# Roots and reciprocals of the heads' norms as columns of 128 tokens x 4, laid out and spread by small DMAs on ScalarE's queue

## The chip, the cores and the metric

The kernel runs on one core of a Trainium2 chip. A core has engines that run side by side, each with its own in-order queue: TensorE (PE; its weight loads are shown as PEld), VectorE (DVE), ScalarE (ACT), GpSimd (POOL) and SyncE (SP, here only for issuing DMAs). Sixteen DMA engines move data between the chip's memory and the core's. The metric is the device time in microseconds of one execution; the profile is of one execution.

## The reference

One sequence of 512 tokens of width 1024 in float32 passes two layers. Each layer is a token mixer and a convolutional FFN, both behind an RMS norm with a shift, a scale and a gate that come from a conditioning vector. Layer 0 mixes by retention, layer 1 by mLSTM, each with 4 heads of width 512. Both end with a norm over each head's 512 values of a token, and here lies the change:

```python
def head_groupnorm(y, g):
    mu = jnp.mean(yf, axis=-1, keepdims=True)
    var = jnp.mean((yf - mu) ** 2, axis=-1, keepdims=True)
    yn = (yf - mu) * lax.rsqrt(var + EPS)
    return yn.reshape(Bt, S, -1) * g
```

In the mLSTM, what is normed is `num / max(|den|, exp(-m_row))` times a sigmoid. A factor per token cancels in the norm except beside EPS, so the kernel norms the numerators alone and adds EPS times the square of the denominator to the variance. Per head and token there is one root and one reciprocal: 512 numbers per head, 8 heads.

## The kernel before

Activations lie transposed, features on the 128 partitions and the 512 tokens along the row. A sum over features is then a matmul with a matrix of ones, and its result comes out repeated on all 128 partitions, as a tile of 128x512. Weights and activations are split in a high and a low part, and each product is three matmuls; the low parts are made by VectorE, or by ScalarE and an accumulating DMA that GpSimd issues (`low_part_added`, L484). Many projections use a seven-product scheme (`seven`, L799), in which each step's result goes through a ScalarE copy into `fs` and a VectorE addition into `p`.

All instructions are first recorded as `Call` objects, then put in order by a planner (`Plan`, L144) and issued, so that nearly every instruction carries the line of `Plan.issue` (L377). The planner simulates the engines with a cost for each instruction (`occ`, the time on its engine; `dma`, the time of a transfer), gives each call a due time worked back from the TensorE instruction that needs it, and for each engine takes the most urgent call that its simulation finds ready. The resulting order of each engine is fixed. Conditioning columns (`side_work`, L457) are loaded into `ada` by SyncE and reduced by VectorE in between.

`heads` (L1296) writes down the order of TensorE's work in a layer's heads, with `q`, `v` and `g` for projections, `s` for the scores, `a` for the attention, `o` for the output projection (four pieces a head, each 24 full matmuls), and `end` for the head's norm. `between` functions put a call after the j-th step of a projection. In `q` and `g` a head has 14 steps of 12 matmuls, in `v` 7 steps of 24. `boundary` (L1046) runs the last pieces in two halves of 256 tokens, so that the next norm can begin. `RET_LAST` and `ML_LAST` (L43) set where the last head's steps stand among the pieces.

`gn_root` (L1285) sums the squares by two matmuls with ones into the bank `pvar`, takes the root (ScalarE) and the reciprocal (VectorE) of the whole 128x512 tile `grs`, and `ret_end` and `ml_end` multiply the head's four tiles `z` by it and split them into `y` (`yh`, `yl`). In an mLSTM head `ml_attend` (L1806) sums the scores into the bank `pden`, and makes from it the tile `den`: absolute value (ScalarE), maximum with `db` (VectorE), square (ScalarE). `db` is one row of `scratch`, a buffer in the chip's memory, spread to 128 partitions by a DMA of SyncE. `bcols` holds another quantity of the gates as columns: 128 tokens on the partitions, 4 columns per head.

Of the kernel before, what the change touches and what calls it, by code (L numbers as in the profile page):

```python
# [16 lines left out]
P = 128  # L17
# [120 lines left out]

class Call:
    __slots__ = ("eng", "name", "obj", "a", "k", "bufs", "preds", "succs", "occ", "lat", "dma", "due", "left", "ready",  # L140
                 "new", "fn", "pin", "after", "end", "shared")


class Plan:  # L144
# [14 lines left out]
    def add(self, eng, obj, name, a, k):  # L159
        c = Call()  # L160
        c.eng, c.obj, c.name, c.a, c.k = eng, obj, name, a, k
        c.preds, c.succs, c.fn, c.pin, c.after = set(), [], None, self.pin, None
        n = len(self.calls)
        views = [(v, m == 0) for m, v in enumerate(a) if isinstance(v, View)]
        views += [(v, key == "accum_out") for key, v in k.items() if isinstance(v, View)]
        c.bufs = list({id(v.buf): v.buf for v, _ in views}.values())
        for v, w in views:
            self.note(n, c, v, w)
        c.dma = 0.0
# [84 lines left out]
        return self.run()  # L254

    def tail(self, c):
        return c.lat if not c.dma else c.dma + (4.5 if "accum_op" in c.k else 3.0)

    def run(self):
        calls = self.calls  # L260
# [58 lines left out]
        while len(out) < len(calls):  # L319
# [61 lines left out]
def trunk(ctx: ExitStack, tc: tile.TileContext, xT, cb, pos, vec, ident, decay, zmask, ada, w_s0, w_in0, w_v0,  # L381
# [811 lines left out]
    class End(Norm):  # L1193
# [24 lines left out]
        def rest(self):  # L1218
# [3 lines left out]
            for k in range(0, KT, 2):  # L1222
                item([], lambda w, k=k: self.use(1, k, k + 2))

    def scores(q, k, hd, weigh, total=None):

        out_s = []
# [54 lines left out]
            V.tensor_tensor(z[:], z[:], ps[:], op=ALU.subtract)  # L1282
        gn_squares(st)

    def gn_root(st, extra=None):  # L1285
        ps = bank("pvar")
        mm2(ps[:], ones["v"][:], st["sum"])
        rs = slot("grs")
        if extra is None:
            reciprocal_root(rs, ps[:], slice(None), eps_t[:])  # L1290
        else:
            V.tensor_tensor(rs[:], ps[:], extra[:], op=ALU.add)
            reciprocal_root(rs, rs[:], slice(None), 0.0)
        st["rs"] = rs

    def heads(st, q, v, s, g, a, mid, end, o, norm, at_last):  # L1296

        def on(fn, i):
            return lambda: item([], lambda w: fn(i))
        S, A_, mid_, end_ = (lambda i, f=f: on(f, i)() for f in (s, a, mid, end))  # L1300
        def at(where, fn, i):
            return lambda j: fn(i) if j == where else None

        q(0)
        q(1, at(6, S, 0))
# [24 lines left out]
    def gate_col(layer, which):  # L1330
        base = (16, 40)[which]
# [193 lines left out]

    def ret_end(i):
        st = R[i]
        gn_root(st)
        st["y"] = []
        for vt in range(4):  # L1530
            z = st["z"][vt]
# [169 lines left out]
                proj_item(w_in0[i * 8 + 2 * n + j], h0, then)  # L1701
        item([], lambda w: sums_early())

    def ret_g(i):
        fold_pairs(pair_srcs(w_in0, i * 8 + 4), sums0.terms, [ret_gate(i)] * 2)

    def ret_v(i, between=nothing):
        fold_values(w_v0[i - 1], sums0.terms, R[i]["v"], center_split, between)
# [6 lines left out]
    def ret_o(i):  # L1715
        if not i:
# [4 lines left out]
    heads(R, ret_q, ret_v, ret_scores, ret_g, ret_attend, lambda i: None, ret_end, ret_o,  # L1721
          ffn0.start, RET_LAST)
# [5 lines left out]
    bcols = fixed(const, [P, 4, H], F32, "bcols")  # L1728
    zm = fixed(const, [P, P], F32, "zm")

    def gates(ps):
# [45 lines left out]

    def ml_scores(i):
        st = M[i]
        mb, db = slot("mb"), slot("db")  # L1780
        S.dma_start(mb[:], scratch[i : i + 1].broadcast_to([P, T]))
        S.dma_start(db[:], scratch[4 + i : 5 + i].broadcast_to([P, T]))

        def weigh(p, ps, J, lo, n):
            w = slot("w")
# [11 lines left out]
        st["db"] = db  # L1797

    def ml_gate(i):
        def then(ps):  # L1800
# [5 lines left out]
    def ml_attend(i):  # L1806
# [6 lines left out]
        gn_sum(st)  # L1813
        ps = bank("pden")
        mm2(ps[:], ones["1"][:], st["sums"])
        d = slot("den")
        A.activation(d[:], ps[:], AF.Abs)
        V.tensor_tensor(d[:], d[:], st["db"][:], op=ALU.max)
        A.activation(d[:], d[:], AF.Square, scale=float(np.sqrt(EPS)))
        st["e2"] = d  # L1820

    def ml_end(i):
        st = M[i]
        gn_root(st, st["e2"])
        st["y"] = []
        for vt in range(4):
            z = st["z"][vt]
# [12 lines left out]
    def ml_g(i):  # L1840
        fold_pairs(pair_srcs(w_in1, 5 + i * 8), start1.sums.terms, [ml_gate(i)] * 2)

    def ml_o(i):
        return pieces(lambda j: w_o1[i, j], 4, gate_col(1, 0), lambda k: M[i]["y"][k], i in O_ADDED)
# [1 line left out]
    def ml_v(i, between=nothing):  # L1846
# [5 lines left out]
    v_items(w_v1, 0, h1, M[0]["v"], plain_split)  # L1852
    item([], lambda w: start1.sums.turn())
    ffn1 = Ffn(1)
    heads(M, ml_q, ml_v, ml_scores, ml_g, ml_attend, lambda i: gn_center(M[i]), ml_end, ml_o,
          ffn1.start, ML_LAST)
    ffn1.items(End())


# [143 lines left out]
```

## Time and profile before

| | |
|---|---|
| median of 3 executions | 1513.67 us |
| lowest, highest | 1513.44, 1513.98 us |
| the profiled execution | 1513.25 us |
| its span, first to last instruction | 1511.3 us |
| granted TensorE clock, mean | 0.994 |

In the profile `DVE RECIPROCAL grs<-grs` names engine, operation, and the tile written and the tiles read; x8 is a count. A row of a busy-time table gives a stretch of time, its length, the busy time and count of instructions of PE, PEld, DVE, ACT and POOL, then the granted TensorE clock (1.00 is full), the busy share of the DMA engines and GB/s. A row of waits reads: who waited, for whom, total us, times, longest. A row of the timeline reads: start, duration, engine, operation, tiles, count, and in brackets the idle time of the engine before it and who ended it. A row of one tile's instructions gives the shortest, median and longest duration in ns and the first and last start. SPq is SyncE issuing DMAs. Matmul rows overlap, since matmuls are pipelined.

### The profile page before, as it was taken

How to read it: one execution, taken by the hardware profiler on the slowest of the kernel's cores; microseconds unless marked ns; L12 is line 12 of the kernel's file. 1: busy time of each engine (PE TensorE's matmuls, PEld its weight loads, DVE VectorE, ACT ScalarE, POOL GpSimd, SP SyncE). 2: the span in 40 equal slices, each digit the busy share in tenths (PEclk: the TensorE clock that was granted, in tenths of full speed). 3: DMA queues.
4: the chain of work that ended last, by engine and by line, in shares of the span. 5: the costliest groups of instructions: out<-in, count | busy, mean ns of one | idle time of the engine just before them, and what ended most of it. 6: DMA issues, size and time to landing. Idle time of an engine off the chain costs nothing.

```text
span 1511.3 us, 27097 instructions
## 1 busy us (share of the span) xinstructions
PE 1477.9 (98%) x10405; PEld 1375.5 (91%) x10405; DVE 1262.9 (84%) x2123; ACT 1069.0 (71%) x1593; POOL 281.6 (19%) x311
## 2 busy tenths in 40 slices
PE   9999999899999999999999999999999999999997
PEld 6889999798998989899998988999989899999997
DVE  6998989676887888888798999999877877877786
ACT  4558858777577666666578986899976867677662
POOL 0234222232111111111001222223131111111100
PEclk9999999999999999999999999999999999999999
DMA  9467999896487999999368887989875868787841
GB/s 375 158 161 204 282 272 275 207 236 148 103 224 202 244 265 255 271 260 253 115 168 223 206 234 202 262 216 248 223 179 136 213 171 196 173 207 182 204 127 56
DMA packets 92979, 314.98 MB, mean 208 GB/s; under 512 B 12193, under 2 KB 14625, under 8 KB 92850
## 3 DMA queue, kind: packets, MB, share of 16 engines
q0 software_dynamic: 31824, 115.88, 41.4%
q1 hardware_dynamic: 61026, 197.38, 36.7%
q8 instruction: 81, 1.33, 0.3%
q14 instruction: 48, 0.39, 0.1%
HBM read 195.23 MB, written 2.12 MB: 131 GB/s over the span
## 4 chain that ended last, share of the span: by engine, by line
PE 85%; DVE 6%; DMA 6%; ACT 2%; issue 1%; POOL 0%; SPq 0%; DVEq 0%; ACTq 0%; POOLq 0%
PE p L377 31%; PE po L377 25%; PE pv L377 9%; PE pp L377 6%; PE pf L377 4%; PE pav L377 4%; PE pst L377 3%; PE psc L377 2%; DMA wb<-w_up 1%; DMA ada<-ada 1%; PE pc L377 1%; ACT whi L377 1%; DVE ws L377 1%; DVE wlo L377 1%; DVE ada L377 1%
## 5 line engine op out<-in xcount | busy, mean ns | idle before, releaser
L377 PE MATMUL p<-hh,whi 128*128 128x256 f32 (+1 forms) x962 | 267.8, 279 | 5.8 <-DVE p L377 5.5
L377 PE MATMUL p<-hl,whi 128*128 128x256 f32 x960 | 266.8, 278 | 0.7 <-DVE hl L377 0.5
L377 PE MATMUL p<-hh,wlo 128*128 128x256 f32 x960 | 265.3, 278 | 1.5 <-DMA wlo<-wa 1.5
L377 ACT ACTIVATE wlo<-whi 128x1024 fp32r<-128x1024 f32 x221 | 233.2, 1059 | 45.5 <-PE po L377 22.0
L377 PEld LDWEIGHTS p<-hh,whi 128*128 128x128 f32 x962 | 181.5, 189 | 7.7 <-DVE p L377 6.0
L377 PEld LDWEIGHTS p<-hl,whi 128*128 128x128 f32 x960 | 181.3, 189 | 1.5 <-DVE hl L377 1.1
L377 PEld LDWEIGHTS p<-hh,wlo 128*128 128x128 f32 x960 | 180.3, 189 | 2.0 <-DMA wlo<-wa 1.9
L377 PE MATMUL p<-t24h,whi 128*128 128x256 f32 x720 | 161.3, 281 | 6.9 <-DVE p L377 4.2
L377 DVE SCALAR_TENSOR_TENSOR x<-po,mod,x 128x512 f32<-128x512 f32 (+1 forms) x184 | 113.6, 629 | 52.5 <-PE po L377 51.7
L377 PE MATMUL po<-ggh,wlo 128*128 128x512 f32 (+1 forms) x448 | 152.6, 343 | 0.8 <-DVE wlo L377 0.8
L377 PE MATMUL po<-ggl,whi 128*128 128x512 f32 (+1 forms) x448 | 153.1, 343 | 0.0
L377 PE MATMUL po<-ggh,whi 128*128 128x512 f32 (+1 forms) x448 | 152.6, 343 | 0.0
L377 ACT CAST whi<-raw 128x1024 fp32r<-128x1024 f32 (+1 forms) x121 | 121.8, 1019 | 26.0 <-PE po L377 7.8
L377 PE MATMUL p<-t24l,whi 128*128 128x256 f32 x480 | 133.6, 278 | 0.0
L377 PEld LDWEIGHTS p<-t24h,whi 128*128 128x128 f32 x720 | 123.0, 189 | 10.8 <-DVE p L377 5.9
L377 DVE SCALAR_TENSOR_TENSOR ada<-ada,c_ext 128x1025 f32<-128x1025 f32 x96 | 122.0, 1275 | 10.4 <-DMA ada<-ada 10.4
L377 POOL DMA_DIRECT2D wlo<-wa x60 | 53.0, 883 | 414.7 <-ACT wlo L377 320.1
L377 PE MATMUL po<-yh,whi 128*128 128x256 f32 (+1 forms) x354 | 116.0, 329 | 0.0
L377 PE MATMUL po<-yl,whi 128*128 128x256 f32 (+1 forms) x352 | 115.7, 329 | 0.0
L377 PE MATMUL po<-yh,wlo 128*128 128x256 f32 (+1 forms) x352 | 115.7, 329 | 0.0
L377 ACT CAST whi<-ws 128x1024 fp32r<-128x1024 f32 x84 | 88.0, 1050 | 30.9 <-DVE ws L377 22.3
L377 DVE TENSOR_TENSOR wlo<-raw,whi 128x768 fp32r<-128x768 f32 (+2 forms) x113 | 101.8, 915 | 7.7 <-ACT whi L377 3.6
(285 smaller groups left out, 4459.8 us busy)
## 6 DMA issues: line engine op xcount, KB each, us to landing
ada<-ada SPq DMA_DIRECT2D x96, 512.5 KB, 6.9
wlo<-ws POOLq DMA_DIRECT2D x71, 512.0 KB, 7.1
wlo<-wa POOLq DMA_DIRECT2D x60, 512.0 KB, 6.7
wlo<-wt POOLq DMA_DIRECT2D x44, 512.0 KB, 7.7
wlo<-raw POOLq DMA_DIRECT2D x40, 512.0 KB, 8.4
wa<-w_up SPq DMA_DIRECT2D x34, 512.0 KB, 5.8
wb<-w_up SPq DMA_DIRECT2D x34, 512.0 KB, 6.8
raw<-w_o SPq DMA_DIRECT2D x32, 512.0 KB, 7.2
```

The source lines that it names most:

```text
L377: getattr(c.obj, c.name)(*[real(v) for v in c.a], **{key: real(v) for key, v in c.k.items()})
```

## The change

The variance is the same on every partition, so one partition's row holds all of it. After the change that row of 512 numbers is cut in four columns of 128 by four DMAs that ScalarE issues (`to_columns`), root and reciprocal work on 128x4, and the result is stored to a line of the chip's memory and spread from there to 128 partitions, both again by DMAs of ScalarE. In a retention head the root stays on the row and only the reciprocal works on columns. In an mLSTM head the denominator takes the same way: absolute value on one row, columns, then maximum with `dcols` (loaded once per layer by SyncE in place of the four spreads `db`) and square on columns.

`gn_root` leaves `ret_end` and `ml_end` and becomes a step `root` of its own in `heads`, placed by `RET_ROOTS`, `ML_ROOTS` and the third of now five numbers in `RET_LAST` and `ML_LAST`; `end` moves later. The last number of `ML_LAST` goes from 2 to 1, so that one piece fewer of the third head runs in halves. The planner is given costs for DMAs of ScalarE (0.1 us of the engine; landing after 2.2 us plus the transfer, and 1.0 us for a DMA that isn't contiguous).

```diff
-RET_LAST = (0, 2, -1, 2)
-ML_LAST = (0, 1, -1, 2)
+RET_ROOTS = (3, 1, 6)
+ML_ROOTS = (-1, -1, -1)
+RET_LAST = (0, 2, 2, 0, 2)
+ML_LAST = (0, 1, -1, 1, 1)
...
-            c.dma = size * (5.4 if "accum_op" in k else 2.45) + 0.05
-            c.occ = 0.9 if eng == "POOL" else 0.4
+            c.dma = size * (5.4 if "accum_op" in k else 2.45) + (1.0 if "allow_slow_non_contiguous" in k else 0.05)
+            c.occ = {"POOL": 0.9, "ACT": 0.1}.get(eng, 0.4)
+            c.near = eng == "ACT"
...
-            if c.dma:
+            if c.near:
+                c.end = t + occ + 2.2 + c.dma
+            elif c.dma:
...
+    def to_columns(row, c):
+        for t in range(4):
+            A.dma_start(c[:, t : t + 1], row[:, t * P : t * P + P], allow_slow_non_contiguous=True)
+
-    def gn_root(st, extra=None):
+    def gn_root(st, n, extra=None):
         ps = bank("pvar")
         mm2(ps[:], ones["v"][:], st["sum"])
         rs = slot("grs")
+        row, c = rs[0:1], columns[:, 4 * n : 4 * n + 4]
         if extra is None:
-            reciprocal_root(rs, ps[:], slice(None), eps_t[:])
+            A.activation(row, ps[0:1], AF.Sqrt, bias=eps_t[0:1])
+            to_columns(row, c)
         else:
-            V.tensor_tensor(rs[:], ps[:], extra[:], op=ALU.add)
-            reciprocal_root(rs, rs[:], slice(None), 0.0)
+            A.copy(row, ps[0:1])
+            to_columns(row, c)
+            V.tensor_tensor(c, c, extra, op=ALU.add)
+            A.activation(c, c, AF.Sqrt)
+        V.reciprocal(c, c)
+        A.dma_start(lines[n].rearrange("(c p) -> p c", p=P), c, allow_slow_non_contiguous=True)
+        A.dma_start(rs[:], lines[n : n + 1].broadcast_to([P, T]))
         st["rs"] = rs
...
         A_(0)
-        v(1, at(3, mid_, 0))
+        v(1, at((3, mid_, 0), (r0, root_, 0)))
         S(1)
-        end_(0)
-        g(1)
+        if r0 < 0:
+            root_(0)
+        g(1, at((12, end_, 0)))
         A_(1)
-        contract_items(o(0))
+        contract_items(o(0), at((r1, root_, 1)))
         mid_(1)
-        q(2)
-        v(2, at(1, end_, 1))
+        q(2, at((6, root_, 1)) if r1 < 0 else nothing)
+        v(2, at((1, end_, 1)))
         S(2)
         g(2)
         A_(2)
-        q(3, at(6, mid_, 2))
-        v(3, at(3, end_, 2))
+        q(3, at((6, mid_, 2), (r2, root_, 2)))
+        v(3, at((0, root_, 2), (4, end_, 2)) if r2 < 0 else at((3, end_, 2)))
         g(3)
         S(3)
-        contract_items(o(1), lambda j: {at_last[0]: A_, at_last[1]: mid_}.get(j, lambda i: None)(3))
+        contract_items(o(1), at(*[(n, f, 3) for n, f in zip(at_last, (A_, mid_, root_))]))
         if at_last[2] < 0:
-            end_(3)
+            root_(3)
         late = o(2)
-        contract_items(late[: 4 - at_last[3]], at(at_last[2], end_, 3))
-        boundary(late[4 - at_last[3] :], o(3), norm)
+        contract_items(late[: 4 - at_last[4]], at((at_last[3], end_, 3)))
+        boundary(late[4 - at_last[4] :], o(3), norm)
...
+            S.dma_start(dcols[:, :, hd], scratch[4 + hd].rearrange("(c p) -> p c", p=P),
+                              allow_slow_non_contiguous=True)
...
-        d = slot("den")
-        A.activation(d[:], ps[:], AF.Abs)
-        V.tensor_tensor(d[:], d[:], st["db"][:], op=ALU.max)
-        A.activation(d[:], d[:], AF.Square, scale=float(np.sqrt(EPS)))
-        st["e2"] = d
+        n = 2 * H + i
+        d, c = slot("den"), columns[:, 4 * n : 4 * n + 4]
+        A.activation(d[0:1], ps[0:1], AF.Abs)
+        to_columns(d[0:1], c)
+        V.tensor_tensor(c, c, dcols[:, :, i], op=ALU.max)
+        A.activation(c, c, AF.Square, scale=float(np.sqrt(EPS)))
+        st["e2"] = c
```

More of the change, by code (lines that the diff above doesn't have):

```diff
@@ L140 @@
     __slots__ = ("eng", "name", "obj", "a", "k", "bufs", "preds", "succs", "occ", "lat", "dma", "due", "left", "ready",
-                 "new", "fn", "pin", "after", "end", "shared")
+                 "new", "fn", "pin", "after", "end", "shared", "near")
 class Plan:
@@ L168, in add @@
             self.note(n, c, v, w)
-        c.dma = 0.0
+        c.dma, c.near = 0.0, False
         width = max([v.width for v, _ in views])
@@ L256, in tail @@
     def tail(self, c):
-        return c.lat if not c.dma else c.dma + (4.5 if "accum_op" in c.k else 3.0)
+        return c.lat if not c.dma else c.dma + (4.5 if "accum_op" in c.k else 2.4 if c.near else 3.0)
     def run(self):
@@ L1223, in rest @@
                 item([], lambda w, k=k: self.use(1, k, k + 2))
+    lines = fixed(dram, [2 * H, T], F32, "lines")
+    columns = fixed(const, [P, 48], F32, "columns")
     def scores(q, k, hd, weigh, total=None):
@@ L1288, in gn_root, with heads, at @@
         rs = slot("grs")
+        row, c = rs[0:1], columns[:, 4 * n : 4 * n + 4]
         if extra is None:
[L1290 to L1293 removed]
+            A.activation(row, ps[0:1], AF.Sqrt, bias=eps_t[0:1])
+            to_columns(row, c)
+        else:
+            A.copy(row, ps[0:1])
[5 more added lines that the diff above has]
+        A.dma_start(rs[:], lines[n : n + 1].broadcast_to([P, T]))
         st["rs"] = rs
[L1296 removed]
+    def heads(st, q, v, s, g, a, mid, root, end, o, norm, roots, at_last):
         def on(fn, i):
             return lambda: item([], lambda w: fn(i))
[L1300 to L1302 removed]
+        S, A_, mid_, root_, end_ = (lambda i, f=f: on(f, i)() for f in (s, a, mid, root, end))
+        def at(*steps):
+            return lambda j: [fn(i) for where, fn, i in steps if j == where]
+        r0, r1, r2 = roots
         q(0)
[L1305 removed]
+        q(1, at((6, S, 0)))
         A_(0)
[L1307 removed]
+        v(1, at((3, mid_, 0), (r0, root_, 0)))
         S(1)
[L1309 to L1310 removed]
+        if r0 < 0:
+            root_(0)
+        g(1, at((12, end_, 0)))
         A_(1)
[L1312 removed]
+        contract_items(o(0), at((r1, root_, 1)))
         mid_(1)
[L1314 to L1315 removed]
+        q(2, at((6, root_, 1)) if r1 < 0 else nothing)
+        v(2, at((1, end_, 1)))
         S(2)
@@ L1527, in ret_end @@
         st = R[i]
-        gn_root(st)
         st["y"] = []
@@ L1702, in ret_q, with ret_g @@
         item([], lambda w: sums_early())
-    def ret_g(i):
-        fold_pairs(pair_srcs(w_in0, i * 8 + 4), sums0.terms, [ret_gate(i)] * 2)
+    def ret_g(i, between=nothing):
+        fold_pairs(pair_srcs(w_in0, i * 8 + 4), sums0.terms, [ret_gate(i)] * 2, between)
     def ret_v(i, between=nothing):
@@ L1720, in trunk @@
     ffn0 = Ffn(0)
-    heads(R, ret_q, ret_v, ret_scores, ret_g, ret_attend, lambda i: None, ret_end, ret_o,
-          ffn0.start, RET_LAST)
+    heads(R, ret_q, ret_v, ret_scores, ret_g, ret_attend, lambda i: None, lambda i: gn_root(R[i], i),
+          ret_end, ret_o, ffn0.start, RET_ROOTS, RET_LAST)
     h1 = []
@@ L1728, in trunk @@
     bcols = fixed(const, [P, 4, H], F32, "bcols")
+    dcols = fixed(const, [P, 4, H], F32, "dcols")
     zm = fixed(const, [P, P], F32, "zm")
@@ L1838, in ml_q, with ml_g @@
         fold_pairs(pair_srcs(w_in1, 1 + i * 8), start1.sums.terms, thens, between)
-    def ml_g(i):
-        fold_pairs(pair_srcs(w_in1, 5 + i * 8), start1.sums.terms, [ml_gate(i)] * 2)
+    def ml_g(i, between=nothing):
+        fold_pairs(pair_srcs(w_in1, 5 + i * 8), start1.sums.terms, [ml_gate(i)] * 2, between)
     def ml_o(i):
@@ L1854, in trunk @@
     ffn1 = Ffn(1)
-    heads(M, ml_q, ml_v, ml_scores, ml_g, ml_attend, lambda i: gn_center(M[i]), ml_end, ml_o,
-          ffn1.start, ML_LAST)
+    heads(M, ml_q, ml_v, ml_scores, ml_g, ml_attend, lambda i: gn_center(M[i]),
+          lambda i: gn_root(M[i], H + i, M[i]["e2"]), ml_end, ml_o, ffn1.start, ML_ROOTS, ML_LAST)
     ffn1.items(End())
```

5 lines of the change are left out of this document (1 added, 4 removed).

## The prediction

> **What bounds the kernel now.** I read the page's busy shares and chain first, then busy time by stage, then who TensorE waited for in those stages.
>
> ```profile
> span 1511.3 us, 27097 instructions
> PE 1477.9 (98%) x10405; PEld 1375.5 (91%) x10405; DVE 1262.9 (84%) x2123; ACT 1069.0 (71%) x1593; POOL 281.6 (19%) x311
> PE 85%; DVE 6%; DMA 6%; ACT 2%; issue 1%; POOL 0%; SPq 0%; DVEq 0%; ACTq 0%; POOLq 0%
> ```
>
> TensorE (PE) carries 85% of the chain and is idle for 1511.3 - 1477.9 = 33.4 us. The change touches no large matmul, so it can only move idle time, in the stages that hold the heads:
>
> ```profile
> core 0: us, PE busy (x) PEld busy (x) DVE busy (x) ACT busy (x) POOL busy (x), PEclk, DMA share, GB/s
> 145.00:345.00 200.00, 192.43 (x1450) 184.02 (x1449) 169.77 (x256) 148.57 (x229) 52.63 (x63) 0.98 0.93 252
> 345.00:421.00 76.00, 76.00 (x498) 69.41 (x498) 55.30 (x102) 48.80 (x78) 12.94 (x14) 1.00 0.58 133
> 850.00:950.00 100.00, 96.66 (x669) 89.58 (x668) 95.93 (x152) 76.53 (x120) 26.25 (x30) 1.00 0.77 200
> 950.00:1100.00 150.00, 148.51 (x1168) 143.38 (x1167) 140.03 (x215) 138.00 (x207) 41.20 (x44) 1.00 0.90 234
> 1100.00:1161.00 61.00, 61.00 (x416) 56.32 (x415) 44.59 (x82) 37.58 (x59) 13.37 (x14) 1.00 0.63 146
> 290.68:297.51 6.83, 5.27 (x23) 4.98 (x23) 3.45 (x7) 2.65 (x4) 2.19 (x2) 0.50 0.70 133
> ```
>
> The first two rows are the retention heads, the next three the mLSTM heads. VectorE (DVE) is 93 to 96% busy in 850 to 1100, ScalarE (ACT) 92% in 950 to 1100, and from 345 to 421 and from 1100 on TensorE has no idle time at all. Who held TensorE, in 145 to 345 (first row) and in 850 to 1161:
>
> ```profile
> PE p L377 <- DVE p L377: 6.2, 2, 5.5
> ...
> PE p L377 <- DMA wlo<-wa: 1.5, 1, 1.5
> PE p L377 <- DVE p L377: 0.7, 1, 0.7
> PE p L377 <- DVE wlo L377: 0.6, 1, 0.6
> PE psc L377 <- DVE mqkl L377: 0.6, 2, 0.4
> PE p L377 <- ACT fs L377: 0.5, 1, 0.5
> ```
>
> One wait of 5.5 us stands out. Its cause, in the chain:
>
> ```profile
> 273.79 13.69 DMA ada<-ada
> ```
>
> A conditioning column loaded for later took 13.7 us to land (DMA share 0.93 in that stage). Its product stood in VectorE's in-order queue ahead of the sum that TensorE needed. The granted clock then was 0.50 for 6.83 us (last row above), about 3.4 us more: 8.9 us for this one accident. The small waits sum to 0.7 (the other wait of the first row) + 3.9 (the five mLSTM rows), with unquoted ones of 0.9, 0.3, 0.2 and 0.2 to 6.2 us. So **at most 8.9 + 6.2 = 15.1 us** are to be had.
>
> **What goes from VectorE.** These rows price it, the last two being the same operations on 128x4 in the start of the kernel:
>
> ```profile
> L377 DVE RECIPROCAL grs<-grs x8: 3342/3349/3353, 161.5 to 1119.8; 128x512 f32<-128x512 f32 x8
> L377 DVE TENSOR_TENSOR grs<-pvar,den x4: 680/682/684, 907.0 to 1116.6; 128x512 f32<-128x512 f32 x4
> L377 DVE TENSOR_TENSOR den<-den,db x4: 679/686/1319, 899.4 to 1100.6; 128x512 f32<-128x512 f32 x4
> L377 ACT ACTIVATE rc<-pms,eps_t x1: 263/263/263, 17.1 to 17.1; 128x4 f32<-128x4 f32 x1
> L377 DVE RECIPROCAL rc<-rc x1: 178/178/178, 17.4 to 17.4; 128x4 f32<-128x4 f32 x1
> ```
>
> Reciprocals: 8 x (3.349 - 0.178) = 25.4 us. Sum and maximum of the mLSTM heads, taken at 0.2 us each on columns: 4 x (0.682 + 0.686 - 0.4) = 3.9 us. VectorE loses 29.3 us, all in the head stages. None of it is TensorE time by itself; its worth is the waits above. Of the 6.2 us of small ones I take half, **-3.1** (bounds 0 and -6.2), since several name VectorE late in a stage where it is 93 to 96% busy, the others a DMA or ScalarE. The 5.5 us accident isn't a lack of VectorE time: a lighter VectorE lands no load sooner. But every instruction's place around it is planned anew: the reciprocal of head 1 leaves from 236 (row below) and the root of head 2 comes in earlier. I take the wait to shrink to the size of the next longest, 1.5 us, after which the clock stayed whole (1.00 in 850 to 950): -(5.5 - 1.5) - 3.4 = **-7.4** (bounds: 0, and -8.9).
>
> ```profile
> 236.01 3.34 DVE L377 RECIPROCAL grs<-grs 128x512 f32<-128x512 f32 x1
> ```
>
> **What comes onto ScalarE.** A retention head issues four column DMAs, one store and one spread, 6 x 4 = 24; an mLSTM head four more for its denominator, 10 x 4 = 40; 64 in all. No row shows ScalarE issuing a DMA. SyncE's rows for the small ones:
>
> ```profile
> L377 SPq DMA_DIRECT2D bcols<-scratch x4: 371/552/938, 808.1 to 819.4; - x4
> L377 SPq DMA_DIRECT2D tab<-decay x4: 328/368/520, 91.9 to 337.1; - x4
> L377 SPq DMA_DIRECT2D scratch<-r_e x1: 265/265/265, 812.7 to 812.7; - x1
> ```
>
> Bounds per issue: 0 (if the queue issues while the engine computes) and 0.94; I take 0.33, between the lowest and the median of these. The 48 column issues stand right behind the activation they read, so ScalarE computes nothing meanwhile: 4 x 0.33 = 1.3 us, where the planner counts 4 x 0.1. Behind them in the same queue wait the copies `fs` and the weight casts that TensorE reads. From 145 to 421 ScalarE has 276 - 197 = 79 us idle, which hides it. In 950 to 1100 it has 150 - 138 = 12 us, and there fall some 16 issues, 5.3 us. The shorter square and root (0.62 and 0.63 to 0.26 each) and the added copy of the variance (0.6) about cancel. Half of 5.3 I put on the path, **+2.7** (bounds 0, and 16 x 0.94 = 15).
>
> SyncE loses four spreads `db` and gains four small `dcols` loads, issued once when the gates are ready and needed some 80 us later (the `bcols` row and the start of the `den` row above): 0. What the new DMAs move is small: 48 columns of 0.5 KB, 8 stores of 2 KB, and 8 spreads of 256 KB for the 4 that go, 1 MB more in all.
>
> **The root's way gets longer.** Instead of one reciprocal of 3.35 us: columns, reciprocal, store, spread, each waiting for the landing before. Landings from issue (min/median/max; first for a 256 KB table like the spread, then for small columns):
>
> ```profile
> DMA to landing us min/median/max: 2.6/5.0/8.8
> ...
> DMA to landing us min/median/max: 2.1/5.0/5.2
> ```
>
> These are SyncE's, behind weight loads; the new queue is empty, so I take 3.65 (middle of 2.1 and 5.2) for columns and store, 5.0 for the spread. In heads 0 to 2 the root moves 2 to 9 items ahead of its use, and an item is 1.4 us or more; what waits is not due. In the last head the way is tight:
>
> ```profile
> 358.88 0.39 PE L377 MATMUL po<-yh,whi 128*128 128x512 f32 x1
> 377.55 0.69 ACT L377 ACTIVATE grs<-pvar,eps_t 128x512 f32<-128x512 f32 x1
> 378.27 3.35 DVE L377 RECIPROCAL grs<-grs 128x512 f32<-128x512 f32 x1 [2.10 <-ACT grs L377]
> 386.78 0.28 PE L377 MATMUL po<-yl,whi 128*128 128x256 f32 x1
> 389.35 1.29 DVE L377 TENSOR_TENSOR yl<-z,yh 128x512 fp32r<-128x512 f32 x2 [0.90 <-ACT yh L377]
> 1119.76 3.34 DVE L377 RECIPROCAL grs<-grs 128x512 f32<-128x512 f32 x1
> 1125.99 2.74 DVE L377 SCALAR_TENSOR_TENSOR yl<-z,vecs,yh 128x512 fp32r<-128x512 f32 x4
> 1127.28 0.28 PE L377 MATMUL po<-yl,whi 128*128 128x256 f32 x1
> ```
>
> A piece of 24 full matmuls takes 5.45 us, a half piece 2.7. Retention: the variance now follows two pieces after 358.9, at 369.8 instead of 375.2. Root done at 372.8 (3.0 after it, as before), last column issued 373.8, landed 377.4, reciprocal 377.6, store 381.3, spread 386.3: 4.7 later than the old 381.6. The last of `y` then ends at 390.6 + 4.7 = 395.3. The last contraction starts after two half pieces at 392.0 and reads that tile at 393.0: 2.3 us late. mLSTM: copy done 1117.3, last column issued 1118.3, landed 1121.9, three small operations 1122.6, store 1126.2, spread 1131.2, 8.1 later than 1123.1; `y` ends 1136.8. With one piece fewer in halves the last contraction starts at 1116.2 + 3 x 5.45 + 2.7 = 1135.3 and reads the tile at 1136.3: 0.5 late. Together **+2.8**; by the least landings 0, by the largest (5.2, 5.2, 8.8) 9.2 + 7.4.
>
> The Trainium skill, "DMA: Bandwidth & Descriptors", section "Anatomy of one DMA", puts a fixed cost of about 2.0 us on each DMA, whatever its size, fitted on GpSimd's path. By it the three steps take some 6 us, the last heads are in time, and the sum would be 2.8 us lower. The trace's 2.1 for the quickest column agrees, its 5.0 at the median doesn't.
>
> The Trainium skill, "TensorE: Matmul & The Clock Gate", section "Part 1: The HAM clock gate", has the clock halved after an idle window of about 3.4 us. This trace agrees at 290.68, after 5.5 us; at 96.12 the clock fell too, though TensorE had worked 4.51 of the 6 us before:
>
> ```profile
> 90.00:96.00 6.00, 4.51 (x34) 3.91 (x33) 5.24 (x13) 4.96 (x11) 0.61 (x1) 1.00 0.25 86
> 96.12:102.95 6.83, 5.18 (x23) 4.59 (x23) 6.83 (x13) 5.06 (x9) 5.29 (x5) 0.50 0.35 112
> ```
>
> By the rule a last-head wait of 2.3 us costs only itself; by that second case it could cost 3.4 more.
>
> **Sum.** -7.4 - 3.1 + 2.7 + 2.8 = -5.0. The profiled execution took 1513.25 us (its span 1511.3 and 1.95 around it), so 1508.25; the median shown is 1513.67, 0.42 higher, so **1508.7**. What a measurement here can tell from no change is about 0.2%, 3 us: 1510.6 to 1516.7 is "the same".
>
> **Rivals.**
> - The accident stays. It is DMA-bound, and less VectorE work leaves the loads as they are. For it: DMA share 0.93. Against: the order there is drawn anew. 1508.7 + 7.4 = 1516.1. Chance 0.22.
> - Slower: in the last heads each landing is at the upper end of the small ones, 5.2, 5.2 and 5.0 for the spread. Retention's spread lands at 389.4, `y` is 5.4 us late, the length after which the clock halved (3.4 more); mLSTM's at 1134.3, 3.6 late. 12.4 instead of 2.8: 1518.3. It decides against the change once the two heads lose over 10.8 us together. For it: the accumulating DMAs of this stage (the share is 0.58 to 0.63); against: an empty queue. Chance 0.16.
> - ScalarE becomes the bound in 950 to 1100: at the median 0.55 per issue, all on the path, 8.8 instead of 2.7: 1514.8. Chance 0.06.
> - All visible idle time goes and nothing comes: 1513.67 - 15.1 = 1498.6. Chance 0.08.
> - That the columns are no cheaper is excluded by the 0.178 row.
>
> **Chances.** The forecast has 0.48, its own range 1504 to 1511.5. Faster: 0.45 of it, 0.08, and 0.02 from the accident staying smaller: 0.55. Same: 0.03, 0.16 of the accident, 0.05 of ScalarE: 0.24. Slower: 0.16, 0.04 and 0.01: 0.21. The range 1499 to 1518.5 takes in all but the outer half of the slower case and of the best one.
>
> **What would show it.** Right: eight reciprocals of 0.18 us, VectorE under 1240 us busy, no wait over 2 us near 286, the clock whole after 103, TensorE idle some 25 us or less. ScalarE's issues show as its own queue's rows near 0.33 us; at 0.1 or below that term is nothing. Waits of `po` on `yl` near 393 and 1136 would show the last heads late; waits on `fs` behind ScalarE's DMA issues, that term. Wrong: a new wait over 5 us anywhere with a halved clock behind it, since one such accident outweighs the whole sum.

## The result and the profile after

The changed kernel takes **1629.74 us** (median of 6 runs, 1624.49 to 1636.84) against 1513.95 us of the kernel before in the same comparison (1513.44 to 1516.14): a ratio of 1.0758, 95% interval 1.0738 to 1.0778. It is slower by 116 us, where 5 us faster were forecast. One execution in the experiments below, of 1835 us at a granted clock of 0.75, is left out of its run's median.

The page of the changed kernel: span, busy time by engine, the small packets, two of the DMA queues (packets, MB, share of 16 engines' span) and the chain by engine. `q10` has no counterpart before; it is ScalarE's.

```profile
span 1635.1 us, 27162 instructions
PE 1508.7 (92%) x10381; PEld 1401.4 (86%) x10381; DVE 1232.1 (75%) x2121; ACT 1067.0 (65%) x1598; POOL 283.0 (17%) x311
DMA packets 106803, 316.08 MB, mean 193 GB/s; under 512 B 25505, under 2 KB 27937, under 8 KB 106674
q0 software_dynamic: 31824, 115.88, 38.6%
q10 hardware_dynamic: 12288, 2.14, 0.8%
PE 60%; DMA 13%; DVE 5%; ACT 3%; issue 3%; ACTq 1%; POOL 0%; SPq 0%; DVEq 0%; POOLq 0%
```

VectorE became lighter as planned: 1262.9 - 1232.1 = 30.8 us. TensorE pays twice. It is idle for 1635.1 - 1508.7 = 126.4 us in place of 33.4, which is 93.0 more, and its own busy time grew by 30.8 us with fewer matmuls: the granted clock was 0.964 on the mean in place of 0.994, and 0.67 and 0.70 in the 7 us after the stops that end at 171 and 233. Together 123.8, the whole difference of the spans. DMA went from 6% of the chain to 13%.

For whom TensorE waited (us in total, times, longest):

```profile
PE p L382 <- ACT fs L382: 30.5, 10, 11.3
PE po L382 <- ACT yh L382: 18.2, 2, 10.0
PE p L382 <- DVE p L382: 16.6, 8, 10.5
PE pav L382 <- ACT sh L382: 12.9, 2, 12.0
PE pmu L382 <- DVE zsl L382: 8.1, 1, 8.1
PE pv L382 <- DMA wlo<-ws: 7.9, 2, 4.1
```

None of the producers named here, ScalarE's copies `fs`, its casts `sh` and `yh`, or VectorE's sums, is one of the new DMAs. `fs`, `sh`, `zsl` and the sums are what stands behind them in the same in-order queues. `yh` is the end of the head's own way: it is made from `z` times the spread `grs`, so there TensorE waits for the landings themselves. Ten waits of 3.8 to 12.0 us sum to 81 us; before, the longest was 5.5.

The landings of the new DMAs (KB each, median us from issue to landing), and below them two rows of the tile `columns`, with the durations as min/median/max in ns.

```profile
grs<-lines ACTq DMA_DIRECT2D x8, 256.0 KB, 5.5
columns<-grs ACTq DMA_DIRECT2D x32, 0.5 KB, 6.2
columns<-den ACTq DMA_DIRECT2D x16, 0.5 KB, 8.3
lines<-columns ACTq DMA_DIRECT2D x8, 2.0 KB, 16.7
```

```profile
L382 ACTq DMA_DIRECT2D columns<-grs x32: 477/616/2662, 150.3 to 1229.7; - x32
L382 DVE RECIPROCAL columns<-columns x8: 171/178/179, 170.0 to 1237.6; 128x4 f32<-128x4 f32 x8
```

The spread of 256 KB lands in 5.5 us, near the 5.0 assumed. The store of 2 KB, a hundredth of it, takes two to three times as long. Its 16.7 us are the median of the three landings that the trace could assign to a store (11.6, 16.7 and 17.2). The spread behind a store can't go before that has landed. In six heads ScalarE stood for it, and by the spread's issue these stores took 10.4 to 17.2 us; with the one of 11.6 us that makes seven, five of them at 10.4 to 11.6. In the eighth ScalarE came to the spread only after 24 us. What that does to ScalarE, in the timeline of ScalarE in the first mLSTM head (start, duration; in brackets the idle time before and what ended it; lines left out between):

```profile
962.55 0.37 ACTq L382 DMA_DIRECT2D lines<-columns  x1
...
966.62 0.40 ACT L382 CAST sh<-sp 128x256 fp32r<-128x256 f32 x1
979.75 0.33 ACTq L382 DMA_DIRECT2D grs<-lines  x1
980.11 1.28 ACT L382 ACT_TABLE_LOAD   x1 [13.09 <-DMA lines<-columns]
...
981.90 0.29 ACT L382 CAST sh<-sp 128x128 fp32r<-128x128 f32 x1
```

ScalarE comes to the spread at 967 and stands there until the store has landed at 979.7. The last `sh`, for which TensorE waits 12.0 us, is behind it in the queue. VectorE does the same at the columns (its timeline in the first retention head):

```profile
158.90 0.69 DVE L382 TENSOR_TENSOR whi<-wb,whi 128x512 fp32r<-128x512 f32 x1 [1.04 <-ACT whi L382]
170.02 0.18 DVE L382 RECIPROCAL columns<-columns 128x4 f32<-128x4 f32 x1 [10.43 <-DMA wa<-w_in]
...
170.75 0.42 DVE L382 TENSOR_TENSOR p<-p,fs 128x256 f32<-128x256 f32 x1
```

The reciprocal waits for four columns issued up to 156.3; the load `wa` named in the bracket is none of its operands, only the last landing that the profile saw. The sum `p` behind it is what TensorE lacks for 10.5 us.

### The profile page after: what moved, and what is told of

Its sections match the earlier page's. It is cut to its first block, busy times and chain, and to the rows that moved or that the text cites. A ratio compares the mean times of both kernels' runs of the same rounds, so it can differ in the third digit from the quotient of the medians.

```text
span 1635.1 us, 27162 instructions
## 1 busy us (share of the span) xinstructions
PE 1508.7 (92%) x10381; PEld 1401.4 (86%) x10381; DVE 1232.1 (75%) x2121; ACT 1067.0 (65%) x1598; POOL 283.0 (17%) x311
## 2 busy tenths in 40 slices
DMA packets 106803, 316.08 MB, mean 193 GB/s; under 512 B 25505, under 2 KB 27937, under 8 KB 106674
## 4 chain that ended last, share of the span: by engine, by line
PE 60%; DMA 13%; DVE 5%; ACT 3%; issue 3%; ACTq 1%; POOL 0%; SPq 0%; DVEq 0%; POOLq 0%
PE p L382 25%; PE po L382 20%; PE pp L382 4%; PE pf L382 4%; PE pv L382 4%; DMA lines<-columns 3%; PE pav L382 2%; DMA columns<-den 2%; DMA wa<-w_in 1%; DMA columns<-grs 1%; DMA grs<-lines 1%; PE psc L382 1%; ACT whi L382 1%; DMA wlo<-ws 1%; DMA wa<-w_up 1%
## 5 line engine op out<-in xcount | busy, mean ns | idle before, releaser
L382 ACT ACTIVATE wlo<-whi 128x1024 fp32r<-128x1024 f32 x221 | 233.1, 1059 | 52.0 <-PE p L382 12.9
L382 PE MATMUL p<-t24h,whi 128*128 128x256 f32 x720 | 168.4, 290 | 30.7 <-DVE p L382 16.3
L382 PEld LDWEIGHTS p<-t24h,whi 128*128 128x128 f32 x720 | 128.2, 197 | 36.0 <-DVE p L382 19.0
L382 PE MATMUL p<-t24l,whi 128*128 128x256 f32 x480 | 137.0, 286 | 0.0
L382 PE MATMUL po<-yh,whi 128*128 128x512 f32 (+1 forms) x346 | 117.5, 341 | 18.2 <-ACT yh L382 18.2
```

Of the source, the lines that this page charges most:

```text
L382: getattr(c.obj, c.name)(*[real(v) for v in c.a], **{key: real(v) for key, v in c.k.items()})
```

## The experiments

The theory after the result: the new DMAs are slow because of their many small packets beside the weight loads, and the in-order queues of ScalarE and VectorE stand at their landings. In each kernel below the planner orders the instructions anew, so small differences can come from the order alone. The two kernels with dummy stores, in packets of 4 and of 16 bytes, are the exception: they have the same order on every engine. The rivals: the steps that were moved, the planner's wrong costs, the added traffic by itself, the longer way of the last heads.

**Only the moved steps.** `root`, `end` and the tuples stand where the change puts them; the arithmetic stays on whole tiles, with no DMA on ScalarE (`db` comes back for `dcols`, not shown).

```diff
-            A.activation(row, ps[0:1], AF.Sqrt, bias=eps_t[0:1])
-            to_columns(row, c)
+            reciprocal_root(rs, ps[:], slice(None), eps_t[:])
...
-        V.reciprocal(c, c)
-        A.dma_start(lines[n].rearrange("(c p) -> p c", p=P), c, allow_slow_non_contiguous=True)
-        A.dma_start(rs[:], lines[n : n + 1].broadcast_to([P, T]))
```

> The new places of the root and of the last heads' pieces, but roots, reciprocals and denominators on the whole 128x512 tiles as before, without any DMA on ScalarE's queue. If the loss of 116 us comes from the new DMAs (the queue theory), this lies near the kernel before, 1505 to 1520 us. If it comes from the moved steps (the place theory), this is slow too, over 1590 us.

Measured: 1511.9 us (1509.77 to 1515.35) against 1515.55, ratio 0.9972 (0.9962 to 0.9983). The moved steps cost nothing; this is the only version that beats the kernel before, if by a quarter of a per cent. Its page and its longest waits:

```profile
PE 1473.6 (97%) x10381; PEld 1371.3 (91%) x10381; DVE 1257.5 (83%) x2121; ACT 1073.9 (71%) x1595; POOL 283.2 (19%) x311
PE p L382 <- DVE p L382: 8.2, 9, 2.2
PE p L382 <- ACT fs L382: 4.1, 4, 1.8
```

No wait is over 2.2 us: the 5.5 us accident of before is gone.

**Only the DMAs.** The reverse: the arithmetic and DMAs of the change, `root` called at the head of `end` in the places of before.

```diff
-RET_LAST = (0, 2, 2, 0, 2)
-ML_LAST = (0, 1, -1, 1, 1)
+RET_LAST = (0, 2, -1, 2)
+ML_LAST = (0, 1, -1, 2)
...
+        def ends(i):
+            root(i)
+            last(i)
```

> The new DMAs with the order of the kernel before: the root right ahead of the head's end, pieces split as before. Queue theory: still slow, 1600 to 1660 us, and worse than the changed kernel if the new places had given room. Place theory: 1515 to 1540 us.

Measured: 1660.78 us, a single run, at the upper edge of what the queue theory allowed. Together with the run before, this puts the loss on the DMAs. The new places win some 31 us of it back: they help, and are not enough.

**Fewer packets.** Token 4p + c in place of 128c + p, so that four neighbouring numbers go to one partition: one column DMA of 128 runs of 16 bytes in place of four of 128 single numbers, and a store of 128 runs in place of 512 numbers. The arithmetic and the bytes are the same; the load of `dcols` is laid out to match (not shown).

```diff
-        for t in range(4):
-            A.dma_start(c[:, t : t + 1], row[:, t * P : t * P + P], allow_slow_non_contiguous=True)
+        A.dma_start(c, row, allow_slow_non_contiguous=True)
...
-        A.dma_start(lines[n].rearrange("(c p) -> p c", p=P), c, allow_slow_non_contiguous=True)
+        A.dma_start(lines[n].rearrange("(p c) -> p c", p=P), c, allow_slow_non_contiguous=True)
```

> Column c of partition p holds token 4p+c instead of 128c+p, so that each partition's four numbers are 16 bytes in a row: the store of a head has 128 packets of 16 bytes instead of 512 of 4, and one DMA of 128 packets lays out the columns instead of four with 512 in all. Places and the planner's costs are those of the changed kernel. Theory of the packets (each packet waits its turn behind a bulk packet on its DMA engine, so the landing goes with their count): the store lands in about 5 us instead of 16.7, and the time is 1515 to 1550 us. Theory of the issue (48 issues at 0.62 us where the planner counts 0.1, some 25 us): 36 issues fewer give back 18 us at most, 1605 to 1615 us. Theory of a fixed latency: nothing but the issues changes, the store still lands after 10 us or more.

Measured: 1543.24 us, ratio 1.0158 (1.0108 to 1.0207). 87 of the 116 us come back. The small packets fall from 25505 to 17249 (before: 12193), and the store's landing from 16.7 to 4.9 us, medians of the three and the two that the trace could assign:

```profile
DMA packets 98547, 316.08 MB, mean 205 GB/s; under 512 B 17249, under 2 KB 19681, under 8 KB 98418
lines<-columns ACTq DMA_DIRECT2D x8, 2.0 KB, 4.9
```

The run takes away 62% of the added packets and three quarters of the column issues together, and makes the packets larger, so it doesn't tell these apart.

**The planner told the truth.** The changed kernel, its planner given the measured issue times and landings (two more lines, not shown, take these in place of the fixed 2.2 us and the transfer).

```diff
+            if c.near:
+                out, src = (v.buf.args[4] for v in a[:2])
+                c.dma, c.occ = (16.7, 0.4) if out == "lines" else (5.5, 0.35) if src == "lines" else (7.0, 0.6)
```

> The changed kernel with the measured costs given to the planner: 7.0 us and 0.6 of the engine for a column, 16.7 and 0.4 for the store, 5.5 and 0.35 for the spread, instead of 3.2, 3.2 and 2.9 with 0.1. The DMAs themselves are unchanged. If the loss is waiting in in-order queues that the planner didn't foresee, other work now stands ahead of each wait and most of it comes back: 1520 to 1570 us, the rest in the last heads, where nothing else is left to do. If the DMAs' own cost on the engines or the places are the cause, it stays over 1600 us.

Measured: 1591.02 us in a single run: 39 us back, which is in neither of the two bands (1520 to 1570, and over 1600). So by this run the waits that the planner didn't foresee are a part of the loss, and not most of it. 16.7 us for a store is also more than most of them took. The largest waits left:

```profile
PE po L385 <- ACT yh L385: 31.4, 3, 10.8
PE p L385 <- DVE p L385: 14.9, 11, 8.0
PE p L385 <- DMA wlo<-wa: 9.8, 3, 8.3
```

Of the three waits on `yh`, of 10.1 to 10.8 us, two are in the last heads and one in the first mLSTM head. The last row is the accumulating DMA of a weight's low part, with no part in the change; issued at 1117.4, it held TensorE up until 1132.1. So the next question is what the small packets do to the loads.

**The stores alone.** The kernel with only the moved steps, and per head a store of 2 KB like that of the change, of numbers nobody reads; nobody waits for it.

```diff
+        d = A.dma_start(lines[n].rearrange("(c p) -> p c", p=P), columns[:, 4 * n : 4 * n + 4], allow_slow_non_contiguous=True)
+        d.after = len(plan.calls) - 2
```

> The kernel with the new places and whole-tile arithmetic (1511.9 us), and in each head, behind the reciprocal, a store of 128x4 numbers as 512 packets of 4 bytes issued by ScalarE as in the changed kernel; nothing reads it and nothing waits for it. Theory of the waits (the loss is made by who waits for the store): within 5 us of 1512. Theory of the traffic (the packets of 4 bytes take turns from the bulk loads, which moved 90 to 213 GB/s during such stores instead of some 240): each store of 10 to 17 us delays weights by several us, 1525 to 1560 us.

Measured: 1535.31 us, ratio 1.0119 (1.0092 to 1.0147): 23 us over the kernel with the moved steps alone, from eight stores of 2 KB. The landing (the median of two, 15.3 and 20.5 us), and the waits that grew:

```profile
lines<-columns ACTq DMA_DIRECT2D x8, 2.0 KB, 17.9
PE p L382 <- DVE p L382: 17.1, 8, 5.5
PE p L382 <- DMA wlo<-wt: 4.7, 2, 3.9
```

**The same stores in runs of 16 bytes.** As above, with `"(p c) -> p c"`: 128 packets in place of 512.

```diff
-        d = A.dma_start(lines[n].rearrange("(c p) -> p c", p=P), columns[:, 4 * n : 4 * n + 4], allow_slow_non_contiguous=True)
+        d = A.dma_start(lines[n].rearrange("(p c) -> p c", p=P), columns[:, 4 * n : 4 * n + 4], allow_slow_non_contiguous=True)
```

> The same dummy stores as in the run of the stores alone, 2 KB per head from ScalarE, nobody waits for them, but each partition writes its four values as one run of 16 bytes: 128 packets in place of 512. Theory (what a store costs beside the weight loads is its number of packets): a quarter of the 23 us that the 4-byte stores cost over the kernel with the new places alone, so 1514 to 1520 us, and landings of some 4 to 6 us. Rival (it is the store itself, its issue and its write to memory, whatever the packets): 1530 to 1540 us as with 4-byte packets.

Measured: 1513.68 us, ratio 0.9992 (0.9968 to 1.0016): 2 us over the moved steps alone, and inside what can't be told from nothing. All engines have the order of the run before, so the 21.6 us between the two are the form of the store, 512 writes of 4 bytes against 128 of 16, and not the store as such; number and size of the packets change together here. The 5.5 us in the waits of the run before aren't from the packets: a wait of 5.3 us for the same sum, behind a late conditioning column, is here too. The landing (the median of three, 4.1 to 9.5 us):

```profile
lines<-columns ACTq DMA_DIRECT2D x8, 2.0 KB, 7.5
```

**The columns alone.** The kernel with the moved steps, plus 48 column DMAs behind the activations as in the change; nobody waits for them. Root and absolute value go to tiles of their own, so that the row isn't overwritten (not shown).

```diff
+        for t in range(4):
+            A.dma_start(c[:, t : t + 1], row[:, t * P : t * P + P], allow_slow_non_contiguous=True)
...
+        to_columns(root[0:1], columns[:, 4 * n : 4 * n + 4])
...
+        to_columns(den[0:1], columns[:, 4 * n : 4 * n + 4])
```

> The same kernel with the 48 column DMAs (4 of 128 packets of 4 bytes behind each root and each absolute value, issued by ScalarE) and whole-tile arithmetic: nothing waits for the columns, except that the row they read stays occupied until they have landed; root and denominator are written to a second tile for that. Theory of the issue (0.62 us each on ScalarE where the planner counts 0.1): 1525 to 1540 us. Theory of the waits: 1512 to 1520 us.

Measured: 1527.81 us (1520.49 to 1530.14; the profile is of the fastest), ratio 1.0076 (1.0056 to 1.0096): 16 us. Here TensorE waits for the copy `fs`, which stands behind the issues on ScalarE: the longest wait, 4.6 us, follows three issues that took 5.0 us together, with ScalarE idle for 4.5. First the wait, then the issue times:

```profile
PE p L382 <- ACT fs L382: 11.1, 10, 4.6
L382 ACTq DMA_DIRECT2D columns<-grt x32: 477/612/2590, 150.1 to 1130.3; - x32
```

**The wait for the store.** The dummy stores of 4-byte packets again, and behind each a read of 128 x 16 numbers of the stored row on ScalarE's queue. Nobody uses what it reads, but it can't be issued before the store has landed. It stands 2 to 8 instructions behind the store.

```diff
+    back = fixed(const, [P, 16], F32, "back")
...
+        A.dma_start(back[:], lines[n : n + 1, 0:16].broadcast_to([P, 16]))
```

> The dummy stores of 4-byte packets again, and behind each a small read of the stored row to 128 x 16 on ScalarE's queue, which nobody reads but which cannot be issued before the store has landed. It stands 2 to 8 instructions behind the store, as the changed kernel's spread does. Theory (a large part of the changed kernel's loss is ScalarE standing at the spread, with the casts and copies for TensorE queued behind it): 8 waits of some 8 to 12 us on ScalarE, of which TensorE pays 3 to 8 us each, so 25 to 65 us over the 1535.3 of the stores alone: 1560 to 1600 us, with TensorE's waits on ScalarE's copies fs and casts. Rival (ScalarE, 65% busy, makes up for the wait, and the rest of the loss is the landings in the heads' own chain): within 10 us of the stores alone, 1530 to 1545 us.

Measured: 1567.64 us, ratio 1.0348 (1.0322 to 1.0373): **32 us** over the stores alone, for a wait whose data no one needs. Its timelines, ScalarE first (three lines), then VectorE:

```profile
155.71 0.39 ACTq L382 DMA_DIRECT2D lines<-columns  x1
...
176.33 0.33 ACTq L382 DMA_DIRECT2D back<-lines  x1
176.71 0.37 ACT L382 COPY fs<-p 128x256 f32<-128x256 f32 x1 [17.45 <-DMA lines<-columns]
```

```profile
159.06 0.88 DVE L382 TENSOR_TENSOR sp<-psc,tab 128x384 f32<-128x384 f32 x2
177.11 0.43 DVE L382 TENSOR_TENSOR p<-p,fs 128x256 f32<-128x256 f32 x1 [17.17 <-ACT fs L382]
```

A store that takes 20.6 us holds ScalarE for 17.5, `fs` waits behind it, VectorE waits for `fs`, and TensorE for VectorE (16.2 us in the waits of this run). The table of waits names VectorE; the cause is two engines back.

**The wait on another queue.** The changed kernel with the spreads issued by SyncE.

```diff
-        A.dma_start(rs[:], lines[n : n + 1].broadcast_to([P, T]))
+        S.dma_start(rs[:], lines[n : n + 1].broadcast_to([P, T]))
```

> The changed kernel with the eight spreads issued by SyncE in place of ScalarE; the stores and columns stay. ScalarE no longer stands at the spread, but SyncE does, with the weight loads queued behind it, and the planner puts the spread into the order of the loads. Theory (the order of the waiting queue is what costs): ScalarE's share comes back, 30 to 60 us, and the loads that stand behind SyncE take some of it away again: 1580 to 1630 us, with waits on weight loads in place of those on fs. Rival (the landings on the head's own way cost, whoever issues): 1620 to 1650 us with TensorE's waits on yh and fs as before.

Measured: 1606.81 us in a single run: 23 us better than the changed kernel, inside the band of the waiting queue and outside that of its rival. The waits on weight loads that were expected with it did not come: the largest row of that kind is 4.4 us in total, against 7.9 in the changed kernel. TensorE's waits:

```profile
PE p L382 <- DVE p L382: 30.2, 11, 11.1
PE po L382 <- ACT yh L382: 22.7, 3, 9.0
PE p L382 <- ACT fs L382: 10.2, 8, 3.1
PE pav L382 <- ACT sh L382: 2.5, 3, 0.9
```

Those on `fs` and `sh` behind the spread fell from 30.5 and 12.9 to 10.2 and 2.5, those of the last heads on `yh` stay, and TensorE waits longer than in the changed kernel for the sums of VectorE. The band of the theory was wide, and one run doesn't say how the rest divides.

**What is left with few packets.** The 16-byte form with the planner told its landings (6.5 us for columns, 5.6 for the store, 5.5 for the spread), and that form with the last head of each layer on whole tiles, as before.

```diff
+                c.dma, c.occ = (5.6, 0.35) if out == "lines" else (5.5, 0.35) if src == "lines" else (6.5, 0.5)
```

> Packets of 16 bytes, with the planner given what those DMAs took: 6.5 us and 0.5 of the engine for the columns, 5.6 and 0.35 for the store, 5.5 and 0.35 for the spread. If what is left of the loss in the 16-byte kernel (28 us) is waits that the planner did not foresee, this falls to 1510 to 1525 us; if it is the longer way of the last heads, it stays at 1525 to 1540 us.

Measured: 1537.1 us, ratio 1.0132 (1.0092 to 1.0173), 6 us less than with the change's costs, within what the two intervals leave open. This is the band of the last heads' longer way.

```diff
     def gn_root(st, n, extra=None):
+        if n % H == H - 1:
+            whole_root(st, extra)
+            return
```

> As the kernel before this one, but the last head of each layer computes root, reciprocal and denominator on the whole tile, as before the change. If the last heads hold the rest of the loss, 1505 to 1513 us, at or below the kernel with the new places alone (1511.9), since six reciprocals of 3.35 us are still off VectorE; if not, no better than the one with columns in all heads.

Measured: 1519.44 us, ratio 1.0022 (1.0007 to 1.0037). The last heads held 18 of the 22 us that remained, but the 1505 to 1513 us expected were not reached. With few packets, true costs and no last head, six reciprocals on columns still give 0.2% slower, while VectorE is 20 us lighter than with the moved steps alone (1237.4 us against 1257.5 busy).

```profile
PE 1479.3 (97%) x10381; PEld 1376.6 (91%) x10381; DVE 1237.4 (82%) x2121; ACT 1070.2 (70%) x1598; POOL 285.9 (19%) x311
```

## Why the prediction was wrong

The sum of the runs, each line over the one above where it adds to it: moved steps alone 1511.9; the stores' packets +23; ScalarE's wait for the store +32; the column DMAs, measured by themselves, +16. That makes 1583.5. The other 46 us up to 1629.7 are left for what none of these four runs has: VectorE waiting for the columns, the heads waiting for the spread, the last heads' longer way. That the parts simply add wasn't tried, and all but the stores' 21.6 us include a new order of instructions.

- **VectorE's term was right.** 29.3 us forecast, 30.8 measured, the reciprocal at 0.178 us as quoted. That it is worth little by itself was right too: in the last run 20 us less of VectorE buy nothing that can be seen.
- **The accident.** Its wait went as forecast: with the moved steps alone TensorE's busy time is 4.3 us less than before, its idle time 4.5 us more. But the spans are equal (1511.5 and 1511.3), since small waits grew in its place; the timed gain is 3.7 us, not 7.4. As the moved steps alone do this, no less VectorE work was needed for it. It was also luck of the order: with the dummy stores, of either form, a wait of 5.3 to 5.5 us of the same kind is back near 300.
- **"These are SyncE's, behind weight loads; the new queue is empty, so I take 3.65" is the step that failed.** An empty queue isn't an idle transfer. 3.65 us were taken for columns and store; the columns took 6.2 and 8.3 at the median, the stores 10.4 to 17.2. The Trainium skill, "DMA: Bandwidth & Descriptors", section "Issuing engines are not separate DMA queues", says that DMAs of all issuing engines run on the same 16 DMA engines and interleave there. The trace agrees: while ScalarE's store of 170.2 was under way, everything together, the loads of the other queues included, moved 28 GB/s (row in the last section).
- **"What the new DMAs move is small" priced bytes.** A column is 128 packets of 4 bytes, a store 512, and each DMA brings 16 more. 48 x 144 + 8 x 528 for columns and stores, 4 x 528 for `dcols` and 16 each for four spreads more make 13312: exactly the rise of the small packets, 12193 to 25505. The Trainium skill, on that page ("DMA: Bandwidth & Descriptors"), section "Rules for kernel authors", has such a strided last dimension lowered to one descriptor per element; this count agrees. Packets, not bytes, were the thing to look at, and where they are written: eight stores, 4224 packets into the chip's memory, slowed the loads, while the columns alone, 6912 packets into the core's own, did not (counts in the last section).
- **"In heads 0 to 2 ... what waits is not due" looked at the wrong instruction.** The root's result was not due. But the spread had to be *issued*, by an in-order queue, after the store had landed. The prediction named what stands behind the column issues and never asked it of the spread. This is the 32 us, shown with data nobody needs.
- **ScalarE's issues.** 0.33 us each were taken, "between the lowest and the median" of SyncE's. Store and spread do take 0.33 to 0.40; columns 0.62 at the median and up to 2.66. The term was +2.7; the columns alone cost 16, packets and all.
- **The last heads.** Forecast 2.3 and 0.5 us late; the chain of the last retention head shows what came:

```profile
408.62 4.91 DMA columns<-grs
...
413.85 10.48 DMA lines<-columns
...
424.36 8.49 DMA grs<-lines
```

  3.65, 3.65 and 5.0 became 4.9, 10.5 and 8.5, so TensorE stood for 10.0 us at 426 and for 8.25 at 1247.
- **The rivals.** The "slower" one had the right mechanism in too few places: 5.2 us per landing and two heads, 1518.3 us. The prediction's sentence that "a new wait over 5 us anywhere with a halved clock behind it" outweighs the whole sum came true with seven such waits, of 8.1 to 12.0 us; in the 7 us after each the granted clock was 0.57 to 0.78 on the mean.

The stops, and the loads beside a store, in windows of the changed kernel (the columns as in the tables of busy time ahead). The first three hold a store under way, the last none:

```profile
414.20:424.40 10.20, 10.20 (x64) 9.12 (x63) 1.01 (x2) 1.06 (x1) 0.85 (x1) 1.00 0.93 90
963.00:979.70 16.70, 7.38 (x54) 6.92 (x53) 5.35 (x9) 4.01 (x8) 2.50 (x3) 0.84 0.90 202
1238.10:1248.10 10.00, 9.15 (x53) 7.88 (x51) 1.77 (x3) 2.11 (x2) 0.86 (x1) 1.00 1.05 186
240.00:300.00 60.00, 58.25 (x473) 56.87 (x472) 53.75 (x89) 46.42 (x72) 18.32 (x22) 1.00 0.92 236
```

With a store under way the DMA engines are as busy as without (0.90 to 1.05 against 0.92) and move 90 to 202 GB/s in place of 236; over the other stores it is 28 to 213. Since the loads waiting there aren't the same in every stage, the runs with dummy stores are the test of this, not these rows.

## What to carry to other kernels

Price a small DMA by its packets, by where it writes them and by what shares the DMA engines at that moment, not by its bytes or by how empty the issuing queue is. Eight stores of single numbers to the chip's memory cost 21.6 us here that the same stores in runs of 16 bytes don't; in the changed kernel, with a quarter of the column issues besides, such runs were worth 87. A DMA that must wait for an earlier one belongs in the list of in-order waits: ask what stands behind it on the *issuing* engine, even where its result isn't due. And where an engine is busy but is not what the others wait for, less work on it buys little: 20 to 30 us less of VectorE showed no gain in any of these kernels, and each new wait of TensorE, 8 to 12 us here with a lower clock behind it, takes back a large part of that.

## What the runs showed of the hardware

- In the changed kernel a store of 512 single numbers took 10.4 to 17.2 us beside weight loads, and up to 20.6 with dummy stores; in runs of 16 bytes the landings that the trace could assign are 4.1 to 9.5.
- In the packet records of the trace a small packet takes 7 to 9 ns at the median. The records of two of the eight stores, at 962.55 and 1161.02, are spread over 12 to 13 us. Those of the other six all lie within 0.4 to 2.7 us and are over 4.5 us after the issue, though five of these stores took 10.4 us or more to land (the sixth is the one nobody stood for). In that time it is the other transfers that are slow. From 171.6 to 180.8, with all packets of the store done, packets of 4 KB of another queue took 1.7 us at the median and up to 8.2; from 240 to 300 it was 0.16 to 0.33 at the median. So the small packets don't just wait for their turn behind large ones: after them the DMA engines read as busy and move little (first row: 0.86 busy at 28 GB/s; the second is a stretch of the store of 962.55 in which TensorE stood: 0.57 and 54).

```profile
170.60:180.80 10.20, 9.35 (x60) 9.15 (x60) 5.37 (x11) 4.80 (x8) 0.00 (x0) 0.75 0.86 28
970.10:977.00 6.90, 0.28 (x3) 0.08 (x1) 0.00 (x0) 0.00 (x0) 0.00 (x0) 0.82 0.57 54
```

- A count over whole traces: slices of half a microsecond in which the DMA engines were over 0.6 busy and moved less than 80 GB/s. They come to 0.5 us before, 3.0 with the moved steps alone, 33.0 with the stores of 4-byte packets, 4.0 with those of 16 bytes, 2.5 with the columns alone and 46.5 in the changed kernel. So many 4-byte writes into the chip's memory hold up the loads, and 4-byte packets as such don't. What holds the engines after the last packet, and whether it is the number or the size of the writes, stays open.
- The Trainium skill, "DMA: Bandwidth & Descriptors", section "Queues, rings and completion order", lets a DMA engine drain some 9 to 17 descriptors of one queue before it turns to the next. An estimate by that: the 32 small descriptors of a store on each engine would need two to four turns. The two stores that are spread over 12 to 13 us look like more turns than that, the other six like few; no run here measured the turns themselves.
